# First and last feature tiles of each FFN input product go whole in three passes; operand sums are made later

## The chip, the cores and the metric

The kernel runs on one core of one Trainium2 chip. The metric is the device time of one execution in microseconds (us). Before the change it is 2356.58 us, the median of 3 runs that lie between 2354.08 and 2357.6.

## The reference

Two layers of a hybrid trunk for 512 tokens of width 1024, batch 1, all in fp32. Each layer holds two SwiGLU feed-forward networks (FFNs) of width 2816, one before and one after a mixing part; the sublayers read the same residual `h`.

```python
def swiglu_ffn(x, w_in, w_out):
    g, u = jnp.split(x @ w_in, 2, axis=-1)      # w_in 1024 x 5632
    return (jax.nn.silu(g) * u) @ w_out         # w_out 2816 x 1024
# per layer
h = h + 0.5 * swiglu_ffn(rms_norm(h, n1), ffn1_w_in, ffn1_w_out)
h = h + mixing(rms_norm(h, n2))                 # SSD heads and latent attention, one output projection
h = h + 0.5 * swiglu_ffn(rms_norm(h, n3), ffn2_w_in, ffn2_w_out)
h = h + sigmoid(rms_norm(h, n4) @ w_g) * (p @ w_p)
```

The change touches `x @ w_in` of the four FFNs and nothing else.

## The kernel before

Activations lie transposed, features on the 128 partitions and the 512 tokens along the free axis, in slots of 128x512 fp32. The residual is eight such slots, `h[0]` to `h[7]`. The factor of the RMS norm (one number per token) is put on after the product, so a product needs only `h` times the gain.

**Three passes.** TensorE multiplies in fp32r, which keeps fewer bits than fp32. Every operand is therefore split into a rounded half `hi` (a cast on ACT) and the rest `lo` (a subtraction on DVE), and each product is the sum of hi·hi, hi·lo and lo·hi: `acc_wx` (L408 to L410) for whole tiles, `product` (L584 to L586) for quarter products.

**Weights.** All weights pass through one list of units in program order. A unit is 128x1024 (512 KB). `load_one` fetches it with a DMA on SP's queue; `split_one` makes `hi` (L290) and `lo` (L291); `weights()` keeps the splits two units ahead of the product that asks. There are 6 raw buffers, 3 for `hi`, 3 for `lo`, 8 PSUM banks and 71 slots.

**Quarter products.** `x @ w_in` goes by a Strassen-Winograd scheme: the tokens are cut into two halves of 256 (`HT`), the 8 tiles of depth into 4 pairs, and four feature tiles (a group) into two pairs. Seven products of 24 matmuls of 128x256 each take the place of eight. The weight operands of products 1, 2 and 3 are quarters as loaded. Those of 5 and 7 are the quarter of 1 or 3 with another quarter added to it: POOL issues an accumulating DMA for that (L304), which waits until the split of the earlier quarter has read the buffer. Those of 6 and 4 come from an addition on DVE (L301). The 22 gate and 22 up tiles make 11 groups: five of gate, five of up, taking turns, and a mixed one, "m", of the last two gate and two up tiles. `ORDER` sets the order of the products of a group; products 7 and 4 of a group come between those of the next.

**Operands of the quarter products.** `NormQ` takes the eight tiles `h[k]` as they become final. For each pair it makes two scaled tiles on ACT (L529), four sums of 128x256 on DVE (L548, L550, L551, L554), and for each of seven operands a `hi` on ACT (L421) and a `lo` on DVE (L422). The running sum of squares for the norm goes beside it (L468, L469); `stats` and `spread` turn it into the factor with a few small matmuls. For layer 0's first FFN the input is transposed on TensorE first (L1453).

**Seams.** At the start of an FFN input product all seven operand families are made while the first products run. At its end, the gated tiles are split for the output product (`split_pair`, again L421 and L422), and the product `"o"` begins with `w_out`.

**Order.** Each engine runs its instructions in one queue, in an order that a scheduler fixed when the kernel was built, from the program order and its own simulation of the times. An instruction that waits holds up everything behind it on its engine. In layer 0 two small loads are read by such instructions early in the kernel: `a_log` by ACT, and `pos_i` by the DVE cast `pf` (L717).

Of the kernel before, what the change touches and what calls it, by code (L numbers as in the profile page):

```python
# [91 lines left out]
def kernel(ctx: ExitStack, tc: tile.TileContext, a: dict, out: bass.AP):  # L92
# [50 lines left out]
    def plan_ffn(i, nm, w_in, w_out):  # L143
        wq = w_in.rearrange("(k two p) f -> two p k f", two=2, p=P)

        def quarter(n, kh, c):
            x, q = GROUPS[n]
            c0 = q * 4 * P
            if x == "m":
                return [(slice(g * P, (g + 1) * P), wq[kh, :, :, g * FF + c0 + c * P:g * FF + c0 + (c + 1) * P])  # L150
                        for g in range(2)]
            c0 += (x == "u") * FF + c * 2 * P
            return [(slice(0, 2 * P), wq[kh, :, :, c0:c0 + 2 * P])]
# [362 lines left out]
    class NormQ(Norm):  # L516

        def __init__(self, *args):  # L520
            super().__init__(*args)
            self.O = {p: [] for p in range(1, 8)}
            self.pair = []

        def add_operand(self, src, operand=True):
            w = self.gain(self.k)
            self.k += 1
            x = S()
            A.activation(x.ap, src, AF.Copy, scale=w)  # L529
            self.pair.append(x)  # L530
            if len(self.pair) == 2:
                e, o = self.pair
                self.pair = []
                self.quarters(e, o)
                slots.put(e, o)

        def quarters(self, e, o):
            a11, a21, a12, a22 = e[:, :HT], e[:, HT:], o[:, :HT], o[:, HT:]
            s, t = S(), S()
            s1, s2, s3, s4 = s[:, :HT], s[:, HT:], t[:, :HT], t[:, HT:]  # L540
# [5 lines left out]
            ready(1, a11)  # L546
            ready(2, a12)
# [8 lines left out]
            ready(4, a22)  # L556
            slots.put(s, t)

        def drop_product(self, p):
            slots.put(*self.O.pop(p))  # L560
# [7 lines left out]
    def ffn(i, nm, norm, nxt, start=lambda: None, tables=lambda: None, between=lambda: None):  # L568

        hid = [[], []]
        NG = len(GROUPS)

        def product(bank, n, p, first):
            hi, lo = weights((i, nm, n, p))
            ops = norm.O[p]
            for k in range(4):
                x = ops[k]
                for f in range(2):  # L580
# [3 lines left out]
                    mm(o, lhsT=hi[:, k, cs], rhs=x[:, :HT], start=first and f == k == 0, stop=False, **more)  # L584
                    mm(o, lhsT=hi[:, k, cs], rhs=x[:, HT:], start=False, stop=False, **more)  # L585
                    mm(o, lhsT=lo[:, k, cs], rhs=x[:, :HT], start=False, stop=f == 1 and k == 3, **more)  # L586
# [7 lines left out]
        def finish(n, a, c, src):  # L594
# [48 lines left out]
        live = {}
        for n in range(NG + 1):
            cur = live[n] = {}
            old = live.get(n - 1)
            if n < NG:
                if GROUPS[n][0] != "u":
                    for a in range(2):
# [864 lines left out]
```

## Time and profile before

| | |
|---|---|
| median of 3 runs | 2356.58 us |
| profiled execution | 2355.45 us, span 2353.7 us, mean granted TensorE clock 0.987 |
| TensorE matmul | 2288.2 us busy, 97% of the span |
| DVE | 1613.9 us, 69% |
| ACT | 1131.5 us, 48% |
| FFN input products | 0 to 250, 765 to 990, 1183 to 1405 and 1921 to 2148 us |

The profiled execution is 1.1 us below the median of the runs. A matmul's busy time is modelled, so a row of matmuls counts as busy from end to end; a stall shows only where a stretch has fewer matmuls than fit in it. The granted clock (PEclk) is 1.00 at full speed and 0.50 at half.

### The profile page before, as it was taken

To read this page: it belongs to the slowest core of one execution; us is meant where nothing else is said; L and a number is where in the kernel's file an instruction comes from. 1 tells how busy PE (TensorE), PEld (TensorE's weight loads), DVE (VectorE), ACT (ScalarE), POOL (GpSimd) and SP (SyncE) were. 2 spreads that over 40 slices of the span, in tenths; PEclk is the share of its full clock that TensorE was granted. 3 is DMA by queue.
4 is the path that set the end of the run, shared out by engine and by line. 5 is a ranking of instruction groups with operands and counts; after the bars stand their busy time and mean duration, and the time that the engine had idled before them with its cause. 6 is when DMAs were issued, how large, how long until landed. Compare 5 with 4: busy or idle time off the path is not lost.

```text
span 2353.7 us, 35460 instructions
## 1 busy us (share of the span) xinstructions
PE 2288.2 (97%) x14118; PEld 2047.7 (87%) x14118; DVE 1613.9 (69%) x2544; ACT 1131.5 (48%) x1861; POOL 242.8 (10%) x232
## 2 busy tenths in 40 slices
PE   7999999999999899999999999999999989999998
PEld 6999888878888899988899988888788879998887
DVE  7777645688666877844687784466876777777345
ACT  6545424454555655532564563254544555455224
POOL 1111000123000111100011110011320001111000
PEclk8999999999999899999999999999999999999999
DMA  5666334311221566543256563342112226665332
GB/s 120 153 135 128 100 94 115 94 51 40 71 62 57 117 135 135 115 117 87 85 126 133 128 127 99 83 118 81 34 48 77 71 54 136 134 135 119 92 86 72
DMA packets 339826, 233.30 MB, mean 99 GB/s; under 512 B 20462, under 2 KB 334028, under 8 KB 339660
## 3 DMA queue, kind: packets, MB, share of 16 engines
q1 hardware_dynamic: 288972, 184.89, 26.6%
q0 software_dynamic: 50688, 46.14, 13.3%
q8 instruction: 111, 1.82, 0.3%
q14 instruction: 55, 0.45, 0.1%
HBM read 228.90 MB, written 2.10 MB: 98 GB/s over the span
## 4 chain that ended last, share of the span: by engine, by line
PE 87%; DVE 5%; issue 3%; DMA 2%; ACT 2%; POOL 1%; SPq 0%; ACTq 0%; POOLq 0%
PE b L408 14%; PE b L410 14%; PE b L409 14%; PE b L584 11%; PE b L585 11%; PE b L586 11%; DMA raw<-in_ffn_w_in_dram 2%; PE b L416 1%; PE b L417 1%; PE b L418 1%; DVE lo L291 1%; ACT hi L290 1%; PE b L1054 1%; DVE s L422 1%; PE b L1219 1%
## 5 line engine op out<-in xcount | busy, mean ns | idle before, releaser
L290 ACT CAST hi<-raw 128x1024 fp32r<-128x1024 f32 (+3 forms) x560 | 549.7, 982 | 838.7 <-PE b L409 380.4
L291 DVE TENSOR_TENSOR lo<-raw,hi 128x1024 fp32r<-128x1024 f32 (+3 forms) x560 | 641.9, 1147 | 434.7 <-ACT hi L290 434.1
L584 PE MATMUL b<-s,hi 128*128 128x256 f32 x2464 | 706.8, 288 | 21.7 <-ACT hi L290 13.0
L585 PE MATMUL b<-s,hi 128*128 128x256 f32 x2464 | 704.9, 287 | 8.1 <-DVE s L422 8.1
L586 PE MATMUL b<-s,lo 128*128 128x256 f32 x2464 | 697.0, 286 | 8.6 <-DVE lo L291 8.6
L408 PE MATMUL b<-s,hi 128*128 128x512 f32 (+1 forms) x1498 | 591.7, 397 | 11.2 <-ACT hi L290 11.2
L410 PE MATMUL b<-s,lo 128*128 128x512 f32 (+1 forms) x1498 | 583.9, 390 | 0.0
L409 PE MATMUL b<-s,hi 128*128 128x512 f32 (+1 forms) x1498 | 583.3, 390 | 0.0
L584 PEld LDWEIGHTS b<-s,hi 128*128 128x128 f32 x2464 | 481.4, 195 | 27.6 <-ACT hi L290 16.0
L585 PEld LDWEIGHTS b<-s,hi 128*128 128x128 f32 x2464 | 482.0, 196 | 10.0 <-DVE s L422 9.3
L586 PEld LDWEIGHTS b<-s,lo 128*128 128x128 f32 x2464 | 477.8, 195 | 9.1 <-DVE lo L291 9.0
L408 PEld LDWEIGHTS b<-s,hi 128*128 128x128 f32 x1498 | 281.3, 188 | 69.1 <-ACT hi L290 12.0
L410 PEld LDWEIGHTS b<-s,lo 128*128 128x128 f32 x1498 | 280.8, 187 | 58.5
L409 PEld LDWEIGHTS b<-s,hi 128*128 128x128 f32 x1498 | 281.2, 188 | 57.7 <-issue 2.9
L304 POOL DMA_DIRECT2D raw<-in_ffn_w_in_dram x96 | 124.0, 1336 | 1003.6 <-DVE lo L291 883.5
L421 ACT CAST s<-s 128x256 fp32r<-128x256 f32 (+1 forms) x304 | 110.7, 416 | 35.5 <-PE b L586 10.7
L422 DVE TENSOR_TENSOR s<-s,s 128x256 fp32r<-128x256 f32 (+1 forms) x304 | 117.5, 432 | 3.6 <-ACT s L421 2.6
L421 ACT CAST s<-b 128x128 fp32r<-128x128 f32 (+2 forms) x196 | 67.2, 361 | 99.7 <-DVE s L422 38.7
L301 DVE TENSOR_TENSOR raw<-raw,raw 128x1024 f32<-128x1024 f32 x88 | 107.6, 1223 | 2.1
L422 DVE TENSOR_TENSOR s<-b,s 128x128 fp32r<-128x128 f32 (+2 forms) x196 | 76.0, 402 | 30.1 <-ACT s L421 28.9
L493 POOL TENSOR_TENSOR nr<-nv,half 128x4 f32<-128x4 f32 (+1 forms) x14 | 16.7, 1190 | 642.4 <-DVE nv L485 639.1
L614 ACT COPY s<-b 128x512 f32<-128x512 f32 x132 | 76.6, 581 | 10.3 <-PE b L586 10.3
(244 smaller groups left out, 2236.1 us busy)
## 6 DMA issues: line engine op xcount, KB each, us to landing
raw<-in_ffn_w_in_dram SPq DMA_DIRECT2D x120, 512.0 KB
raw<-in_ffn_w_in_dram POOLq DMA_DIRECT2D x80, 512.0 KB, 5.8
raw<-in_ffn_w_out_dram SPq DMA_DIRECT2D x64, 512.0 KB
raw<-in_w_in_mix_dram SPq DMA_DIRECT2D x50, 512.0 KB
raw<-in_w_out_mix_dram SPq DMA_DIRECT2D x32, 512.0 KB
raw<-in_ffn_w_out_dram SPq DMA_DIRECT2D x32, 384.0 KB
raw<-in_w_ple_gate_dram SPq DMA_DIRECT2D x16, 512.0 KB
raw<-in_ffn_w_in_dram SPq DMA_DIRECT2D x24, 256.0 KB
```

What stands on the lines that cost most here:

```text
L290: A.copy(hi[:, :n], x[:, :n])
L291: V.tensor_tensor(lo[:, :n], x[:, :n], hi[:, :n].bitcast(F32), op=ALU.subtract)
L301: V.tensor_tensor(x[:, :n], x[:, :n], loaded[add][:, :n], op=ALU.add)
L304: lambda dst, src: G.dma_start(out=dst, in_=src, accum_op=ALU.add))
L408: mm(b, lhsT=hi[:, kk, cs], rhs=xh, start=st, stop=False)
L409: mm(b, lhsT=hi[:, kk, cs], rhs=xl, start=False, stop=False)
L410: mm(b, lhsT=lo[:, kk, cs], rhs=xh, start=False, stop=en)
L421: A.copy(hi, src)
L422: V.tensor_tensor(lo, src, hi.bitcast(F32), op=ALU.subtract)
L584: mm(o, lhsT=hi[:, k, cs], rhs=x[:, :HT], start=first and f == k == 0, stop=False, **more)
L585: mm(o, lhsT=hi[:, k, cs], rhs=x[:, HT:], start=False, stop=False, **more)
L586: mm(o, lhsT=lo[:, k, cs], rhs=x[:, :HT], start=False, stop=f == 1 and k == 3, **more)
```

## The change

Of the 22 gate and 22 up tiles, eight no longer go by quarter products. Gate tiles 0 to 3 go first, each "whole": 24 matmuls of 128x512 with `acc_wx`, from a weight unit of eight depth tiles by 128 columns. The last two gate and two up tiles (20 and 21) go whole at the end, in turn with products 7 and 4 of the last group. Nine groups of quarter products stay, and the mixed group is gone. The first group now runs 1, 5, 2, 3, 6 rather than 1, 2, 5, 3, 6.

For the whole tiles the eight `h[k]` are split as they are (`hi` on ACT, `lo` by one DVE operation of 128x512, now L457). Operands 1, 2 and 4 are plain halves of these tiles, so they need nothing more. Operands 5, 3, 6 and 7 are made from `h` by `sums`, called once after each of the four first whole tiles. In the changed kernel, the lines are L418 to L420 for whole tiles, L591 to L593 for quarter products, L300 and L301 for the weight splits, L431 and L432 for the halves, L538 and L547 to L553 in `sums`.

```diff
+GROUPS = [("u", 0)] + [(x, q) for q in range(1, KF // 4) for x in "gu"]
+NG = len(GROUPS)
+LAST = KF // 4 * 4
+
+FIRST_ORDER = ((1, 0), (5, 0), (2, 0), (3, 0), (6, 0))
 ORDER = ((1, 0), (2, 0), (7, 1), (5, 0), (4, 1), (3, 0), (6, 0))
-GROUPS = [(x, q) for q in range(KF // 4) for x in "gu"] + [("m", KF // 4)]
...
+        def whole(x, f):
+            unit((i, nm, x, f), KD, P, (None, kview(w_in, 0, KD, (x == "u") * FF + f * P, P)))
+
+        for f in range(4):
+            whole("g", f)
+        for n in range(NG):
+            for p, back in ORDER if n else FIRST_ORDER:
+                quarter_unit(n - back, p)
+        quarter_unit(NG - 1, 7)
+        whole("g", LAST)
+        quarter_unit(NG - 1, 4)
+        whole("g", LAST + 1)
+        whole("u", LAST)
+        whole("u", LAST + 1)
...
-            self.O = {p: [] for p in range(1, 8)}
-            self.pair = []
-
-        def add_operand(self, src, operand=True):
...
+            self.O = {p: [] for p in (5, 3, 6, 7)}
+
+        def sums(self, j):
+            e, o, s, t = S(), S(), S(), S()
+            for k, x in ((2 * j, e), (2 * j + 1, o)):
+                A.activation(x.ap, h[k].ap, AF.Copy, scale=self.gain(k))
...
-            ready(1, a11)
-            ready(2, a12)
             V.tensor_tensor(s1, a21, a22, op=ALU.subtract)
             ready(5, s1)
...
-            ready(4, a22)
-            slots.put(s, t)
+            slots.put(e, o, s, t)
+
+        def operand(self, p, k):
+            if p in self.O:
+                y = self.O[p][k]
+                return y[:, :HT], y[:, HT:]
+            odd, half = {1: (0, 0), 2: (1, 0), 4: (1, 1)}[p]
+            hi, lo = self.X[2 * k + odd]
+            ts = slice(half * HT, (half + 1) * HT)
+            return hi[:, ts], lo[:, ts]
...
+        for f in range(4):
+            held.append((f, whole("g", f)))
+            if f == 0:
+                start()
+                norm.stats()
+            if f == 2:
+                norm.spread()
+            if f >= 2:
+                while held:
+                    evac(*held.pop(0))
+            norm.sums(f)
...
+        product(ba, NG - 1, 7, False)
+        combined(NG - 1, 1, 1, ba, cur["n5"], ALU.subtract, swap=True)
+        presplit(1)
+        g = [whole("g", LAST)]
+        presplit(2)
+        product(ba, NG - 1, 4, False)
+        finish(NG - 1, 1, 0, ba.ap)
```

`whole` in `ffn` takes a bank and runs `acc_wx` on the unit; `evac` multiplies a bank by the norm's factor into the gated tiles and puts SiLU on them.

**How the order moves, first place: TensorE at the start of layer 0's second FFN.** In these rows `b` is a PSUM bank, `s` an operand slot, `hi` and `lo` a weight's halves. Before, the last whole-tile product of the mixing part (L410) is followed by quarter products 1 and 2:

```order
L410 MATMUL b_282_7725<-s_489_7482,lo_7560 128x512
L408 MATMUL b_282_7725<-s_489_7482,hi_7559 128x512
L409 MATMUL b_282_7725<-s_490_7483,hi_7559 128x512
L410 MATMUL b_282_7725<-s_489_7482,lo_7560 128x512
L584 MATMUL b_283_7775<-s_496_7529,hi_7630 128x256
L585 MATMUL b_283_7775<-s_496_7529,hi_7630 128x256
L586 MATMUL b_283_7775<-s_496_7529,lo_7631 128x256
L584 MATMUL b_283_7775<-s_496_7529,hi_7630 128x256
```

Now (bank `b_285` is gate tile 0, `b_287` tile 1, `b_288` tile 2) three whole tiles share the first operand slots as these come ready:

```order
L418 MATMUL b_285_7475<-s_494_7351,hi_7381 128x512
L418 MATMUL b_287_7537<-s_489_7304,hi_7429 128x512
L419 MATMUL b_287_7537<-s_490_7305,hi_7429 128x512
L419 MATMUL b_285_7475<-s_495_7352,hi_7381 128x512
L420 MATMUL b_285_7475<-s_494_7351,lo_7382 128x512
L418 MATMUL b_285_7475<-s_496_7372,hi_7381 128x512
L419 MATMUL b_285_7475<-s_497_7373,hi_7381 128x512
L420 MATMUL b_285_7475<-s_496_7372,lo_7382 128x512
L418 MATMUL b_285_7475<-s_498_7399,hi_7381 128x512
L418 MATMUL b_288_7590<-s_489_7304,hi_7478 128x512
L419 MATMUL b_288_7590<-s_490_7305,hi_7478 128x512
```

The matmuls became twice as wide and reuse each operand three times before a quarter product is reached.

**Second place: ACT at the end of layer 0's first input product.** Before, `hi_2880` is the weight of product 7 of the mixed group, `hi_2920` that of product 4, `hi_2968` the first unit of the output product:

```order
L290 CAST hi_2880<-raw_2527 128x1024
L421 CAST s_156_3042<-s_110_2203 128x256
L421 CAST s_156_3042<-s_112_2205 128x256
L421 CAST s_154_2998<-s_111_2204 128x256
L290 CAST hi_2920<-raw_2364 128x1024
L421 CAST s_152_2996<-s_109_2202 128x256
L421 CAST s_152_2996<-s_111_2204 128x256
L421 CAST s_160_3057<-s_119_2658 128x256
L421 CAST s_158_3044<-s_110_2203 128x256
L421 CAST s_158_3044<-s_112_2205 128x256
L290 CAST hi_2968<-raw_2592 128x1024
```

Now `hi_2495` is the weight of product 7 of the last group (it reads what the accumulating DMA leaves), `hi_2525` that of whole gate tile 20:

```order
L300 CAST hi_2495<-raw_2195 128x1024
L431 CAST s_145_2787<-s_97_1645 128x256
L431 CAST s_145_2787<-s_99_1647 128x256
L608 ACTIVATE s_108_2098<-s_108_2098 128x512
L431 CAST s_132_2685<-s_86_1192 128x256
L431 CAST s_132_2685<-s_88_1194 128x256
L300 CAST hi_2525<-raw_2258 128x1024
```

The cast for product 7 is followed by casts for product 4 and the four whole tiles, and no longer by the output product's.

**Third place: DVE at the start of layer 0.** Before, the cast `pf` stands directly ahead of the weight split `lo_338` of product 5:

```order
L422 TENSOR_TENSOR s_47_288<-s_43_281,s_47_288 128x256
L422 TENSOR_TENSOR s_39_259<-s_33_242,s_39_259 128x256
L422 TENSOR_TENSOR s_52_307<-s_43_281,s_52_307 128x256
L551 TENSOR_TENSOR s_45_284<-s_43_281,s_44_283 128x256
L717 CAST pf_800<-pos_i 4x128
L291 TENSOR_TENSOR lo_338<-raw_97,hi_337 128x1024
```

Now the split of gate tile 2 (`lo_247`) stands ahead of it, and the next split behind it is that of gate tile 3:

```order
L301 TENSOR_TENSOR lo_247<-raw_222,hi_246 128x1024
L547 TENSOR_TENSOR s_44_387<-s_42_385,s_43_386 128x256
L479 TENSOR_TENSOR s_33_300<-s_33_300,tmp_302 128x512
L432 TENSOR_TENSOR s_38_339<-s_36_334,s_38_339 128x256
L432 TENSOR_TENSOR s_40_347<-s_36_334,s_40_347 128x256
L549 TENSOR_TENSOR s_44_387<-s_44_387,s_42_385 128x256
L432 TENSOR_TENSOR s_39_344<-s_37_335,s_39_344 128x256
L479 TENSOR_TENSOR s_33_300<-s_33_300,tmp_305 128x512
L553 TENSOR_TENSOR s_66_517<-s_63_514 128x256
L775 CAST pf_934<-pos_i 4x128
```

`pf` has moved from behind the splits of two quarter products to behind those of three whole tiles.

More of the change, by code (lines that the diff above doesn't have):

```diff
@@ L147, in quarter @@
             x, q = GROUPS[n]
[L148 to L152, printed above, removed]
+            c0 = q * 4 * P + (x == "u") * FF + c * 2 * P
             return [(slice(0, 2 * P), wq[kh, :, :, c0:c0 + 2 * P])]
@@ L639, in presplit, with whole @@
                 q = len(H) // 2
-                if q < done[0] and len(slots.free) - 4 - (KF - len(hid[0]) * 2) >= KEEP:
+                if q < done[0] and len(slots.free) - 4 - (LAST - len(hid[0]) * 2) >= KEEP:
                     split_pair(q)
[L643 to L649, printed above, removed]
-                        hid[a] += [S() for _ in range(1 if GROUPS[n][0] == "m" else 2)]
-                ba = cur["a"] = B()
-                product(ba, n, 1, True)
-                cur["m1"] = copied(ba)
-                bc = B()
-                product(bc, n, 2, True)
-                if n:
+        def whole(x, f):
+            b = B()
+            acc_wx(b.ap, weights((i, nm, x, f)), norm.ops)
+            return b
@@ new lines, in ffn, with evac @@
+        held = []
+        def evac(f, b):
+            q, fs = f // 2, slice(f % 2 * HT, (f % 2 + 1) * HT)
+            if f % 2 == 0:
+                for a in range(2):
+                    hid[a].append(S())
+            for a in range(2):
+                ts = slice(a * HT, (a + 1) * HT)
+                V.tensor_tensor(hid[a][q][:, fs], b[:, ts], norm.rb[:, ts], op=ALU.mult)
+            banks.put(b)
+            if f % 2:
+                for a in range(2):
+                    A.activation(hid[a][q].ap, hid[a][q].ap, AF.Silu)
@@ new lines, in ffn @@
+        for f in range(4):
[9 more added lines that the diff above has]
+            norm.sums(f)
+        cur = {}
+        for n in range(NG):
+            old, cur = cur, {}
+            if GROUPS[n][0] == "g":
+                for a in range(2):
+                    hid[a] += [S(), S()]
+            for p, back in ORDER if n else FIRST_ORDER:
+                if p == 1:
+                    ba = cur["a"] = B()
+                    product(ba, n, 1, True)
+                    cur["m1"] = copied(ba)
+                elif p == 2:
+                    bc = B()
+                    product(bc, n, 2, True)
@@ L690, in ffn, with split_last @@
+        def split_last():
+            for f in range(2):
+                t, hi, lo = hid[f].pop(), S(F32R), S(F32R)
+                halves(t.ap, hi.ap, lo.ap)
+                slots.put(t)
+                H[LAST + f] = hi, lo
         for m in range(KD):
@@ L695, in ffn @@
                 if m == 0:
-                    while len(H) < k0 + nk:
+                    while len(H) < min(k0 + nk, LAST):
                         split_pair(len(H) // 2)
+                    if k0 + nk == KF:
+                        split_last()
                 acc_wx(b.ap, w, {f: (p.ap, q.ap) for f, (p, q) in H.items()}, k0, k0 == 0, k0 + 8 >= KF)
```

103 lines of the change are left out of this document (44 added, 59 removed).

## The prediction

> **What bounds the kernel now.** First the page: busy shares, the chain, the clock by slices.
>
> ```profile
> PE 2288.2 (97%) x14118; PEld 2047.7 (87%) x14118; DVE 1613.9 (69%) x2544; ACT 1131.5 (48%) x1861; POOL 242.8 (10%) x232
> PE 87%; DVE 5%; issue 3%; DMA 2%; ACT 2%; POOL 1%; SPq 0%; ACTq 0%; POOLq 0%
> ```
>
> TensorE sets the time almost everywhere. Two prices therefore matter: that of a matmul in a full stretch, and that of the stretches that are not full. The view by windows gives both (columns: window in us, then length, busy time and count of each engine, granted clock, DMA share, GB/s).
>
> ```profile
> 810.00:980.00 170.00, 170.00 (x1419) 170.00 (x1418) 129.99 (x146) 88.32 (x117) 23.11 (x18) 1.00 0.62 134
> 300.00:360.00 60.00, 60.00 (x266) 49.71 (x265) 24.21 (x28) 16.93 (x21) 0.00 (x0) 1.00 0.35 94
> ```
>
> The first lies inside an FFN input product and holds 256-wide matmuls: 170/1419 = 0.1198 us each, with nothing lost. The second is an output product: 60/266 = 0.2256 us per 512-wide matmul. The steady state has nothing to give. These are the eight seams, the starts and the ends of the four input products:
>
> ```profile
> 14.00:82.00 68.00, 54.69 (x407) 52.75 (x406) 52.59 (x101) 40.55 (x71) 6.55 (x6) 0.90 0.49 113
> 765.00:805.00 40.00, 32.30 (x223) 30.87 (x223) 36.16 (x69) 27.55 (x53) 3.60 (x3) 0.83 0.49 107
> 1183.00:1203.00 20.00, 17.53 (x136) 16.36 (x135) 15.55 (x25) 11.51 (x19) 4.09 (x4) 1.00 0.52 97
> 1920.00:1961.00 41.00, 32.99 (x224) 31.66 (x223) 36.94 (x70) 28.20 (x55) 3.87 (x4) 0.83 0.47 105
> 222.00:270.00 48.00, 43.62 (x322) 41.86 (x322) 38.30 (x66) 27.88 (x55) 6.47 (x5) 0.96 0.54 120
> 985.00:1013.00 28.00, 24.75 (x166) 23.04 (x165) 23.77 (x45) 14.68 (x32) 2.61 (x2) 0.94 0.57 141
> 1390.00:1426.00 36.00, 30.14 (x200) 28.32 (x200) 27.80 (x52) 17.99 (x39) 2.59 (x2) 0.91 0.39 96
> 2140.00:2170.00 30.00, 25.42 (x174) 23.68 (x173) 25.03 (x46) 15.05 (x32) 2.62 (x2) 0.94 0.55 132
> ```
>
> A seam's loss is its length less its matmuls at 0.1198. Starts: 68 - 407 x 0.1198 = 19.2; likewise 13.3, 3.7 and 14.2; together 50.4 us. The ends also hold the output product's first 512-wide matmuls; these are the rows of its hi·hi line (L408) alone in the same windows:
>
> ```profile
> 222.00:270.00 48.00, 3.62 (x9) 1.89 (x10) 0.96 0.54 120
> 985.00:1013.00 28.00, 3.63 (x9) 1.70 (x9) 0.94 0.57 141
> 1390.00:1426.00 36.00, 4.14 (x10) 1.98 (x10) 0.91 0.39 96
> 2140.00:2170.00 30.00, 3.35 (x8) 1.51 (x8) 0.94 0.55 132
> ```
>
> Three passes each make 27, 27, 30 and 24 wide matmuls. Loss of the first end: 48 - 295 x 0.1198 - 27 x 0.2256 = 6.6; the others 5.3, 8.9 and 6.6; together 27.4. **All seams lose 77.8 us.** That is the pot from which any gain must come.
>
> Two causes fill it. In layer 0's start, the queues of ACT and DVE stand still for small loads (timeline; idle time before and its releaser in brackets; then the window behind it):
>
> ```profile
> 27.03 0.22 ACT L843 ACTIVATE d_a<-a_log 128x16 f32<-128x16 f32 x1 [4.37 <-DMA a_log<-in_a_log_dram]
> 29.76 0.21 ACT L843 ACTIVATE d_a<-a_log 128x16 f32<-128x16 f32 x1 [1.91 <-DMA a_log<-in_a_log_dram]
> 30.64 0.21 DVE L717 CAST pf<-pos_i 4x128 f32<-4x128 int32 x1 [6.34 <-DMA pos_i<-in_positions_dram]
> 32.05 0.58 PE L586 MATMUL b<-s,lo 128*128 128x256 f32 x1 [7.83 <-DVE lo L291]
> 32.00:41.40 9.40, 8.87 (x40) 8.56 (x41) 7.89 (x18) 2.48 (x4) 1.29 (x1) 0.50 0.35 53
> ```
>
> The weight split that TensorE needs is queued behind `pf`, so TensorE idles 7.83 us and then runs at a granted clock of 0.50 for over 9 us: 40 matmuls in 9.40 us are 0.235 each, nearly twice the pitch. In the second FFN of both layers the operand families are the cause:
>
> ```profile
> 765.00:775.00 10.00, 6.15 (x29) 5.41 (x29) 10.00 (x25) 8.99 (x23) 0.00 (x0) 0.67 0.53 106
> 775.00:785.00 10.00, 6.65 (x47) 6.25 (x46) 10.00 (x23) 6.67 (x15) 0.00 (x0) 0.84 0.16 52
> ```
>
> DVE is busy 10.00 of 10 us while TensorE gets through 29 and 47 matmuls of the 83 that fit.
>
> **The change: columns.** Each FFN loses 2 x 7 x 24 = 336 matmuls of 256 (11 groups to 9) and gains 8 x 24 = 192 of 512. 192 x 0.2256 - 336 x 0.1198 = 43.3 - 40.2 = 3.06 us, times four: **+12.2 us**, certain, as TensorE is the bound.
>
> **Starts of the second FFNs.** What DVE must do before product 5, from the groups of 757 to 793 us, the kernel-wide group of L447 (count | busy us, mean ns), that window's DVE time, and the first and last starts of two lines:
>
> ```profile
> L422 DVE TENSOR_TENSOR s<-s,s 128x256 fp32r<-128x256 f32 x28 | 10.4, 417 | 0.0
> L291 DVE TENSOR_TENSOR lo<-raw,hi 128x1024 fp32r<-128x1024 f32 x7 | 8.5, 1217 | 0.0
> L1289 DVE TENSOR_TENSOR s<-b,s 128x512 f32<-128x512 f32 x8 | 5.1, 684 | 5.1 <-PE b L410 5.1
> L469 DVE TENSOR_TENSOR s<-s,tmp 128x512 f32<-128x512 f32 x7 | 4.8, 683 | 0.0
> L301 DVE TENSOR_TENSOR raw<-raw,raw 128x1024 f32<-128x1024 f32 x2 | 2.4, 1214 | 0.0
> L554 DVE TENSOR_TENSOR s<-s 128x256 f32<-128x256 f32 x4 | 1.7, 419 | 0.0
> L548 DVE TENSOR_TENSOR s<-s,s 128x256 f32<-128x256 f32 x4 | 1.7, 418 | 0.0
> L550 DVE TENSOR_TENSOR s<-s,s 128x256 f32<-128x256 f32 x4 | 1.7, 417 | 0.0
> L551 DVE TENSOR_TENSOR s<-s,s 128x256 f32<-128x256 f32 x4 | 1.7, 416 | 0.0
> L619 DVE TENSOR_TENSOR s<-b,s 128x512 f32<-128x512 f32 x1 | 0.7, 682 | 0.0
> L447 DVE SCALAR_TENSOR_TENSOR s<-s,vec,s 128x512 fp32r<-128x512 f32 x32 | 24.1, 752 | 22.2 <-ACT s L446 22.2
> 757.00:793.00 36.00, 34.26 (x69) 0.81 0.35 73
> L1289 DVE TENSOR_TENSOR s<-b,s x8: 681/682/693, 756.6 to 767.4; 128x512 f32<-128x512 f32 x8
> L584 PE MATMUL b<-s,hi x4: 277/281/384, 765.1 to 767.1; 128*128 128x256 f32 x4
> ```
>
> After: 8 residual updates at 0.684, 7 weight splits at 1.217, 8 `lo` of whole tiles at 0.752, 7 squares' sums at 0.683, 16 sums of 256 and 16 `lo` of 256 at 0.417, in all 38.1 us. Neighbours overlap: the 69 instructions of the window add up to 38.7 us by their groups and occupy 34.26, a factor 0.885, so 33.7 us. The cover on TensorE is the rest of the mixing product (the first update starts at 756.6, the first quarter product at 765.1: 8.5), 96 whole matmuls (21.7) and product 1 (2.9): 33.1 us. So DVE is about level with TensorE where it was far behind. What stays: the order above takes three whole tiles in turn, so the `hi` casts of tiles 2 and 3, behind `h` and square work on ACT, come some 2.4 and 1.4 us late. Product 5 now runs second, and its weight needs an accumulating DMA behind product 1's split: 5.8 to 7.6 us to landing in this place now,
>
> ```profile
> DMA to landing us min/median/max: 5.8/7.6/7.6
> ```
>
> so cast and split end 2.4 to 4.2 us after TensorE is ready for it; I take 3.3. With 1.4 for half clock (between 0 and the 3.3 that 10 us at 0.67 lose now): **8.5 us for each such start, against 13.3 and 14.2**; 4 if the waits lie under each other, 13 if DVE runs later than its sum.
>
> **Start of layer 0.** SP's order keeps the small loads in the same place, so `pf` still ends near 30.6. Only gate tile 3's split is now queued behind it, not product 5's. Tiles 0 to 2 give TensorE 72 x 0.2256 = 16.2 us from 14 on, to about 30. Tile 3's cast, on ACT behind both `a_log` waits, ends near 33 and its `lo` near 36: a stall of 5 to 6 us in place of 7.8, and some half clock after it. I take **10 against 19.2**; 6 if the casts slip through, 14 if the half clock lasts as it does now. **Layer 1's first FFN** has its last output tiles as cover and no `pos_i`: 1.5 (0 to 3) against 3.7.
>
> **The ends.** Now TensorE finishes 7, then 4, then needs the output product's `hi`, behind pairs that are split late; the longest waits there:
>
> ```profile
> PE b L408 <- ACT hi L290: 11.2, 4, 4.1
> 242.00:252.00 10.00, 8.27 (x55) 7.87 (x54) 10.00 (x21) 3.87 (x9) 2.60 (x2) 0.83 0.59 99
> ```
>
> After, 96 whole matmuls give 21.7 us in which the pairs are split, so that wait goes. What is late next is tile 20: on ACT its cast stands behind product 7's, which waits for the accumulating DMA. Counted from the start of product 5 on TensorE: product 3's `lo` ends at 2.5, the DMA lands 5.8 to 7.1 later (8.6 to 9.9 with its issue), tile 20's `lo` ends at 14 to 15.2. Products 5, 4, 3, 6 (4 x 24 x 0.1198 = 11.5) and none else run till then, so TensorE waits 2.5 to 3.7 us less what tile 20's first passes may do on `hi` alone: 2 to 3.2, say 2.6. The window 242 to 252 shows the clock at 0.83 although its longest wait is 1.1 us, a loss of 1.7, of which I take half, 0.9: **3.5 us for each end, 14 for four, against 27.4** (0.8 each with an early landing and full clock; 5 with 3.2 of wait and the whole 1.7).
>
> [...]
>
> **Sum.** Starts 10 + 8.5 + 8.5 + 1.5 = 28.5, ends 14: 42.5 of the 77.8 remain, a gain of 35.3; less 12.2 for columns: -23.1. The profiled execution's 2355.45 us becomes 2332.4; with the 1.1 by which the median is above it, **2333 us**. Costed at nothing: SP loads 35 weight units of 512 KB per FFN in place of 33, POOL 18 in place of 22, so fewer bytes in all, and the DMA share in the steady windows is at most 0.62; operands hold 32 slots in place of 28 (8 tiles and 4 families of four, before 7 families), which could only delay pair splits, and these have 21.7 us of cover.
>
> **Rivals.**
>
> *The seams close.* The low ends: 6 + 4 + 4 + 0 for the starts, 0.8 each at the ends, 17.2 remain: 2356.6 + 12.2 - 60.6 = 2308. For it: 21.7 us of cover at both sides is more than any wait. Against it: ACT and DVE queues are fixed, and a cast behind a DMA waits whatever the cover.
>
> *Slower: the late accumulating DMA in front of tile 20.* Place: ACT's cast of product 7 at the four ends. The DMA waits for product 3's `lo` on DVE, which is 10.00 of 10 busy there now. If pair splits (L431, L432) run ahead of that `lo` and it comes 6 us later, TensorE waits 2.6 + 6 and then pays a clock window of 3.4: 12 us per end. Total 28.5 + 48 = 76.5 remain, the gain is 1.3 and the time 2367. It decides from 9.3 us per end on: (77.8 - 12.2 - 28.5)/4. Against it: in DVE's order two pair splits stand shortly ahead of that `lo`, and eight between it and product 7's.
>
> *No change.* The ends keep their 27.4 because the DMA holds them, the second FFNs' starts their 27.5 because DVE is as full as now; only layer 0 and the short start gain, 11.4 against 12.2: 2357.
>
> **Chances.** Forecast (own range 2318 to 2349, from the ends of its terms) 0.62; seams close 0.20; slower 0.12; no change 0.06. The 80% range must take in half of the second case and the fourth: 2311 to 2357 leaves out about 0.1 below and 0.1 above. What a measurement here can tell from no change is 0.2%, 4.7 us. Faster 0.82, same 0.06, slower 0.12.
>
> **What would show it.** In the profile after: some 194 us of 256-wide matmuls per FFN at 0.12 and 192 wide ones at 0.226, or the 12.2 is wrong. `pf` near 30.6 with a wait of 5 to 6 us on `lo` before it ends, or layer 0's term is. DVE near 10 of 10 from 757 to 790 with TensorE above 8 of 10, or the level sum is. At the ends, one wait of 2 to 3 us of L418 on ACT's `hi` and none at the output product; a wait over 9 us there would make the prediction wrong.

## The result: 0.7% faster, and where the time went

The changed kernel takes 2338.9 us in the median of 8 runs (2333.85 to 2346.76); the kernel before takes 2354.52 us in 8 runs beside them (2353.15 to 2357.75). The ratio is 0.9934, 95% interval 0.9917 to 0.9951: 15.6 us faster by the medians, where a gain of 23 (2333 from 2356.6) was forecast. The runs of the changed kernel spread over 13 us, those of the kernel before over 5. The profiled execution is the second longest of the eight, 2346.55 us with a span of 2344.9, so in it the change is worth only 8.8 us. That will matter below.

The page of the changed kernel: busy shares, the chain of waits and the transfers.

```profile
span 2344.9 us, 34036 instructions
PE 2295.8 (98%) x13542; PEld 2021.8 (86%) x13542; DVE 1552.6 (66%) x2456; ACT 1093.3 (47%) x1780; POOL 215.5 (9%) x208
...
PE 81%; issue 10%; DVE 4%; DMA 2%; ACT 2%; POOL 1%; SPq 1%; POOLq 0%; ACTq 0%; DVEq 0%
...
raw<-in_ffn_w_in_dram SPq DMA_DIRECT2D x140, 512.0 KB
raw<-in_ffn_w_in_dram POOLq DMA_DIRECT2D x72, 512.0 KB, 5.9
```

TensorE is still the bound, DVE and ACT have less to do, and POOL makes its 72 accumulating loads. The list of TensorE's waits says what it waits for now:

```profile
PE b L591 <- ACT hi L300: 9.9, 6, 4.5
PE b L418 <- ACT hi L300: 7.8, 7, 1.9
PE b L420 <- DVE lo L301: 6.5, 7, 1.9
PE b L591 <- ACT s L608: 6.4, 6, 2.5
```

The list of the kernel before was led by thirteen waits of quarter products for ACT's casts, the output product's waits for them, and waits for DVE's `lo`, of which product 5's at layer 0's start was 7.8 us:

```profile
PE b L584 <- ACT hi L290: 13.0, 13, 2.6
PE b L408 <- ACT hi L290: 11.2, 4, 4.1
PE b L586 <- DVE lo L291: 8.6, 2, 7.8
```

The output product's waits and the long one of product 5 at layer 0 are gone, and of the first kind six are left, one of them 4.5 us long. New are short waits of the whole tiles (L418, L420) and, in the fourth row, waits of a quarter product that no seam explains.

To see where the difference lies, every profile here was put into the same ledger. For each matmul the time to the next one's start, less its pitch (0.1198 us for 256 columns, 0.2256 for 512), is its loss; the losses are added up over the starts, the middles and the ends of the four input products. (The windows are somewhat wider than the prediction's, so the kernel before stands here at 56 + 29 rather than 50 + 27.)

| loss in us | starts | middles | ends | elsewhere | all | span less loss |
|---|---|---|---|---|---|---|
| before | 56.3 | 1.2 | 29.2 | 83.9 | 170.3 | 2183.4 |
| changed | 37.6 | 12.2 | 15.0 | 84.8 | 149.4 | 2195.5 |
| difference | -18.7 | +11.0 | -14.2 | +0.9 | -20.9 | +12.1 |

-20.9 + 12.1 = -8.8, the difference of the spans. So the columns cost 12.1 us, the two kinds of seam gave 32.9 back, and **11 us appeared in a place where the kernel before lost next to nothing: the middle of the input products**. Two windows of the changed kernel show it, the middle of layer 0's and of layer 1's first FFN:

```profile
75.00:215.00 140.00, 140.00 (x1169) 140.00 (x1168) 110.90 (x137) 73.31 (x99) 18.00 (x14) 1.00 0.61 132
1200.00:1370.00 170.00, 164.25 (x1346) 163.03 (x1345) 123.92 (x140) 83.09 (x108) 20.55 (x16) 0.99 0.56 121
```

140/1169 is 0.1198 us per matmul, the full pitch. In the second window 1346 matmuls ran where 1419 fit: 73 x 0.1198 = 8.7 us are lost. Six groups there lose 0.4 to 1.2 us each in one wait, at full clock. A seventh loses 2.65 us at 1349 us, and behind it the granted clock is 0.50 for the 3.4 us from 1352.2 to 1355.7, another 1.7 us. TensorE's waits in that window:

```profile
PE b L591 <- ACT s L608: 4.5, 4, 2.5
PE b L591 <- DVE s L620: 1.3, 3, 0.6
```

Both releasers are work that stands on ACT and DVE behind a late weight. The group of ACT's weight casts in the same window, with what ended the idle time before them:

```profile
L300 ACT CAST hi<-raw 128x1024 fp32r<-128x1024 f32 x57 | 59.6, 1047 | 72.5 <-PE b L592 36.3 <-DMA raw<-in_ffn_w_in_dram 28.4 <-issue 7.4
```

The casts wait 28.4 us for loads; in the same product of the kernel before they waited 4.5 us:

```profile
L290 ACT CAST hi<-raw 128x1024 fp32r<-128x1024 f32 x66 | 69.1, 1049 | 86.0 <-PE b L585 66.5 <-issue 8.0 <-DMA raw<-in_ffn_w_in_dram 4.5
```

From the view of the accumulating loads there, first of the kernel before, then of the changed one:

```profile
DMA to landing us min/median/max: 4.5/5.8/6.2
```

```profile
DMA to landing us min/median/max: 5.7/6.7/8.2
```

POOL's timeline has the reason one step further back (start, length, idle time before). First the changed kernel in the undisturbed middle of layer 0's first FFN, then in layer 1's:

```profile
132.79 1.28 POOL L314 DMA_DIRECT2D raw<-in_ffn_w_in_dram  x1 [13.00 <-DVE lo L301]
138.66 1.28 POOL L314 DMA_DIRECT2D raw<-in_ffn_w_in_dram  x1 [4.58 <-DVE lo L301]
152.91 1.28 POOL L314 DMA_DIRECT2D raw<-in_ffn_w_in_dram  x1 [12.97 <-DVE lo L301]
...
1226.28 1.28 POOL L314 DMA_DIRECT2D raw<-in_ffn_w_in_dram  x1 [14.88 <-DVE lo L301]
1230.86 1.28 POOL L314 DMA_DIRECT2D raw<-in_ffn_w_in_dram  x1 [3.30 <-DVE lo L301]
1247.12 1.28 POOL L314 DMA_DIRECT2D raw<-in_ffn_w_in_dram  x1 [14.98 <-DVE lo L301]
```

Each group issues two accumulating loads, for product 7 of the group before and for product 5. In these groups of layer 0 they start 5.9 us apart, about the time one takes to land (median 5.9 us there). In layer 1 they start 4.4 to 4.7 us apart in seven groups running, so the second is under way with the first and takes 7.9 to 8.2 us to land; the casts of the second begin up to 8.3 us after its start rather than 6.0. And the group takes 20.6 to 21.2 us, once 22.2, where it takes 20.1 in layer 0 (152.91 - 132.79).

### The profile page after: what moved, and what is told of

Same layout as the page of the kernel before. It is cut to its first block, busy times and chain, and to the rows that moved or that the text cites. A ratio compares the mean times of both kernels' runs of the same rounds, so it can differ in the third digit from the quotient of the medians.

```text
span 2344.9 us, 34036 instructions
## 1 busy us (share of the span) xinstructions
PE 2295.8 (98%) x13542; PEld 2021.8 (86%) x13542; DVE 1552.6 (66%) x2456; ACT 1093.3 (47%) x1780; POOL 215.5 (9%) x208
## 4 chain that ended last, share of the span: by engine, by line
PE 81%; issue 10%; DVE 4%; DMA 2%; ACT 2%; POOL 1%; SPq 1%; POOLq 0%; ACTq 0%; DVEq 0%
PE b L418 15%; PE b L420 15%; PE b L419 15%; PE b L591 7%; PE b L593 7%; PE b L592 7%; DMA raw<-in_ffn_w_in_dram 2%; PE b L427 2%; PE b L426 2%; PE b L428 2%; DVE lo L301 1%; PE b L1112 1%; ACT hi L300 1%; PE b L1277 1%; DVE s L432 1%
## 5 line engine op out<-in xcount | busy, mean ns | idle before, releaser
L301 DVE TENSOR_TENSOR lo<-raw,hi 128x1024 fp32r<-128x1024 f32 (+3 forms) x536 | 612.4, 1143 | 469.6 <-ACT hi L300 469.0
L300 ACT CAST hi<-raw 128x1024 fp32r<-128x1024 f32 (+3 forms) x536 | 523.8, 979 | 855.6 <-PE b L419 411.5
L418 PE MATMUL b<-s,hi 128*128 128x512 f32 (+1 forms) x1754 | 693.5, 397 | 7.8 <-ACT hi L300 7.8
L420 PE MATMUL b<-s,lo 128*128 128x512 f32 (+1 forms) x1754 | 685.8, 392 | 6.5 <-DVE lo L301 6.5
L419 PE MATMUL b<-s,hi 128*128 128x512 f32 (+1 forms) x1754 | 683.8, 390 | 0.0
L591 PE MATMUL b<-s,hi 128*128 128x256 f32 x2016 | 574.4, 286 | 18.0 <-ACT hi L300 9.9
L592 PE MATMUL b<-s,hi 128*128 128x256 f32 x2016 | 572.0, 284 | 0.0
L593 PE MATMUL b<-s,lo 128*128 128x256 f32 x2016 | 567.9, 285 | 1.7 <-DVE lo L301 1.7
L591 PEld LDWEIGHTS b<-s,hi 128*128 128x128 f32 x2016 | 390.1, 193 | 23.5 <-ACT hi L300 11.7
L418 PEld LDWEIGHTS b<-s,hi 128*128 128x128 f32 x1754 | 330.6, 188 | 77.4 <-ACT hi L300 10.7
L420 PEld LDWEIGHTS b<-s,lo 128*128 128x128 f32 x1754 | 329.9, 188 | 77.6 <-DVE lo L301 8.8
L592 PEld LDWEIGHTS b<-s,hi 128*128 128x128 f32 x2016 | 390.2, 194 | 0.2
L593 PEld LDWEIGHTS b<-s,lo 128*128 128x128 f32 x2016 | 387.2, 193 | 2.6 <-DVE lo L301 2.5
L419 PEld LDWEIGHTS b<-s,hi 128*128 128x128 f32 x1754 | 330.5, 188 | 68.0 <-issue 2.9
L314 POOL DMA_DIRECT2D raw<-in_ffn_w_in_dram x72 | 92.8, 1289 | 850.5 <-DVE lo L301 819.2
L431 ACT CAST s<-b 128x128 fp32r<-128x128 f32 (+2 forms) x196 | 67.2, 361 | 99.8 <-DVE s L432 38.7
L431 ACT CAST s<-s 128x256 fp32r<-128x256 f32 (+1 forms) x248 | 94.2, 423 | 36.8 <-DVE s L611 13.2
L432 DVE TENSOR_TENSOR s<-s,s 128x256 fp32r<-128x256 f32 (+1 forms) x248 | 100.2, 442 | 9.8 <-PE b L593 7.4
L432 DVE TENSOR_TENSOR s<-b,s 128x128 fp32r<-128x128 f32 (+2 forms) x196 | 75.9, 401 | 30.2 <-ACT s L431 29.1
L426 PE MATMUL b<-hi,s 128*128 128x512 f32 (+1 forms) x208 | 78.5, 377 | 0.0
```

The lines of the kernel that those rows point to most:

```text
L300: A.copy(hi[:, :n], x[:, :n])
L301: V.tensor_tensor(lo[:, :n], x[:, :n], hi[:, :n].bitcast(F32), op=ALU.subtract)
L314: lambda dst, src: G.dma_start(out=dst, in_=src, accum_op=ALU.add))
L418: mm(b, lhsT=hi[:, kk, cs], rhs=xh, start=st, stop=False)
L419: mm(b, lhsT=hi[:, kk, cs], rhs=xl, start=False, stop=False)
L420: mm(b, lhsT=lo[:, kk, cs], rhs=xh, start=False, stop=en)
```

## The experiments

### The same kernel, a second profile

No edit.

> The changed kernel, unaltered, looked at once more. In its first profile 13 us were lost in the middle of the input products (9.1 of them in layer 1's first FFN, about 1 us per group), where the kernel before loses nothing. Theory (a): this is a matter of timing between the two accumulating DMAs of a group, a state that a product falls into or not. Then another execution has the loss at another FFN or nowhere, and the time goes with it: about 2334 without it, 2346 with it. Rival (b): it is built into the order of layer 1's first FFN. Then the 9 us come back at the same place.

Measured: 2346.58 us, 149.5 us of loss in all, as it happens the same total. But it lies elsewhere: the middles lose 1.1, 1.9, 3.3 and 1.3 us rather than 0.3, 1.5, 9.0 and 1.4, and the ends 18.7 rather than 15.0. The start of layer 1's first FFN sets its pairs of loads 4.4 to 4.8 us apart again, with this landing time there:

```profile
DMA to landing us min/median/max: 5.8/6.0/8.0
```

So the close spacing comes back at the same place, which favours (b), and its price only in part (3.3, not 9.0), which favours (a). Both expectations had a part right: the spacing belongs to this kernel at this place, and how long the loads then take varies from one execution to the next (median 6.0 us here, 6.7 in the first profile). The time, though, did not fall with the loss in the middle as (a) had it.

### Product 5 third, not second

```diff
-FIRST_ORDER = ((1, 0), (5, 0), (2, 0), (3, 0), (6, 0))
+FIRST_ORDER = ((1, 0), (2, 0), (5, 0), (3, 0), (6, 0))
```

> The first group runs products 1, 2, 5, 3, 6 as it did before the change; all else as changed. Theory: product 5's accumulating DMA is late because it stands second (waits of 4.7 and 4.0 us at the starts of the second FFNs, 1.2 and 0.9 in layer 0); with product 2's 2.9 us ahead of it the starts lose 3 us less in each second FFN and 1.5 less in layer 0, some 7 us in all: 2332. If that late start is also what sets off the loss in the middle, that goes too and the runs lie close together near 2327. Rival: DVE's sums and splits are as late as the DMA, product 2 only takes the wait over: 2338 to 2340.

Measured: 2336.22 us against 2359.2 of the kernel before, ratio 0.9912 (0.989 to 0.9934), runs from 2330.31 to 2347.69. In its profile (2332.11 us) the starts lose 31.2 us (37.6 before this edit), 6.4 less, and the middles 1.0 in all. POOL's timeline in layer 1's first FFN:

```profile
1199.27 1.28 POOL L314 DMA_DIRECT2D raw<-in_ffn_w_in_dram  x1 [11.62 <-DVE lo L301]
1205.03 1.28 POOL L314 DMA_DIRECT2D raw<-in_ffn_w_in_dram  x1 [4.47 <-DVE lo L301]
1219.53 1.28 POOL L314 DMA_DIRECT2D raw<-in_ffn_w_in_dram  x1 [13.22 <-DVE lo L301]
1225.30 1.28 POOL L314 DMA_DIRECT2D raw<-in_ffn_w_in_dram  x1 [4.49 <-DVE lo L301]
```

The loads start 5.8 us apart from the first group on. So product 5 in second place is what sets the close spacing at this place. The 6.4 us at the starts are near the 7 expected, but they can't be put down to this edit: the next two kernels, which keep product 5 second, lose 33 and 29.9 us at their starts. And this kernel's list has waits that the changed kernel's doesn't have, for the norm's factor from POOL and from DVE, so the rival, that product 2 only takes the wait over, is right in part:

```profile
PE b L513 <- POOL nr L503: 5.4, 2, 4.0
PE b L591 <- DVE nv L495: 3.1, 1, 3.1
```

The narrow spread was not found: the runs lie 17 us apart, and the interval overlaps the changed kernel's. By the times this run does not decide what the order is worth.

### Whole tiles 20 and 21 ahead of products 7 and 4

```diff
-        quarter_unit(NG - 1, 7)
         whole("g", LAST)
-        quarter_unit(NG - 1, 4)
+        quarter_unit(NG - 1, 7)
         whole("g", LAST + 1)
+        quarter_unit(NG - 1, 4)
```

(and the same in `ffn`, where the products are issued).

> At the end of each input product whole gate tile 20 goes before product 7, and tile 21 before product 4; all else as changed. Theory: the waits of 1.0 and 1.1 us at each end come from tile 20's cast standing behind product 7's, which waits for its DMA. Now 5.4 us of tile 20 cover that DMA: the ends lose 7 instead of 14.5 us, 2332. Rival: tile 20's own weights or the pair splits are what is late, and the waits stay: 2339.

Measured: 2325.75 us, ratio 0.986 (0.9843 to 0.9877). The ends lose 1.2 us in all, 0.3 each, where 7 was expected and the changed kernel has 15.0. These are the waits of TensorE from 185 to 240 us, first of the changed kernel, then of this one:

```profile
PE b L420 <- DVE lo L301: 1.0, 1, 1.0
PE b L418 <- ACT hi L300: 0.9, 1, 0.9
```

```profile
PE b L591 <- ACT s L431: 0.6, 1, 0.6
```

And its window at that end:

```profile
205.00:240.00 35.00, 34.40 (x239) 32.10 (x238) 31.50 (x56) 24.81 (x49) 1.28 (x1) 1.00 0.53 135
```

The two short waits are gone. The granted clock was 0.95 in the changed kernel's window from 215 to 250 us and is 1.00 here. So at the ends nearly the whole cost was the cast of product 7 ahead of tile 20's. Nearly twice the expected gain came: the stalls at the four ends (8.9 us in the changed kernel, counted from start to start) went, and the half clock behind two of them (3.4 us) with them. The middles still lose 6.8 us, with the loads of layer 1's first FFN 4.4 to 4.7 us apart in its first groups: the edit at the ends does not touch them.

### The first half of the change alone

Gate tiles 0 to 3 whole at the start; the last four tiles by the mixed group, as before the change.

```diff
-GROUPS = [("u", 0)] + [(x, q) for q in range(1, KF // 4) for x in "gu"]
+GROUPS = [("u", 0)] + [(x, q) for q in range(1, KF // 4) for x in "gu"] + [("m", KF // 4)]
...
-        whole("g", LAST)
...
-        whole("u", LAST + 1)
```

> Only the first half of the change: gate tiles 0 to 3 whole at the start, operand sums made later; the last four tiles go by the mixed group as before the change. Columns then cost 96 x 0.2256 - 168 x 0.1198 = 1.5 us per FFN in place of 3.1. Theory: starts and ends are worth what the ledger says, 15 us at the starts and 13 at the ends. So this kernel gains 6 us of columns back and loses 13 at the ends: about 2346. Rival: the ends gain nothing of their own and follow from the starts: 2333.

Measured: 2341.06 us, ratio 0.9925 (0.9912 to 0.9938). Span less loss is 2334.9 - 145.7 = 2189.2, so the columns cost 5.8 us here (6.1 expected, 12.1 with the whole change). The ends lose 25.5 us, 10.5 more than in the changed kernel. That is the theory's side: the ends do not follow from the starts. The middles lose 7.7, and the starts 29.9, 7.7 less than in the changed kernel with the same first group. Product 5's load at the second FFNs' starts landed after 7.5 and 8.1 us here and after 10.4 and 9.7 there; why it did, no run explains. By the times the second half of the change, as it was written, is worth nothing that can be told (0.9925 against 0.9934): its 10.5 us at the ends pay for its 6.3 us of columns and little more.

### Product 5's quarter by a plain load

```diff
+                if p == 1:
+                    at[n, "b"] = raw(4, 256, *quarter(n, 0, 1))
...
-(at[n, before][0], quarter(n, 0, 1) if add is None else at[n, add][1])))
+(at[n, before][0], at[n, "b"] if p == 5 else quarter(n, 0, 1) if add is None else at[n, add][1])))
```

The order 1, 5, 2, 3, 6 is kept. Product 5's second quarter comes on SP's queue and is added on DVE; only product 7 has an accumulating load left.

> The changed kernel, order 1, 5, 2, 3, 6 kept, but product 5's second weight quarter comes by a plain load on SP and an addition on DVE; only product 7 keeps an accumulating DMA. Theory: the loss in the middle (12 us in one profile, 8 in another) comes from the two accumulating DMAs of a group when they are issued 4.7 us apart and so overlap (landing up to 8 us), which then repeats from group to group; 5.9 us apart, they don't. With one such DMA per group the middle loses 1 us or less in all, and product 5's wait at the second FFNs' starts (4.7, 4.0) falls below 2: about 2322 to 2328, and DVE has 9 additions of 1.22 us more per FFN, which it has room for (77% busy in the middle). Rival: the loss comes from ACT's and DVE's queues, whatever feeds them; then the middle still loses 5 us or more, and the additions make it worse: 2340 or above.

Measured: 2316.33 us, ratio 0.9836 (0.9822 to 0.9849). The middles lose 0.8 us, the second FFNs' starts 4.5 each (12.0 and 11.8 in the changed kernel), the ends 13.3. The two middles (the second is layer 1's first FFN):

```profile
75.00:215.00 140.00, 140.00 (x1169) 140.00 (x1168) 119.99 (x148) 73.73 (x103) 8.98 (x7) 1.00 0.52 132
1190.00:1340.00 150.00, 150.00 (x1252) 150.00 (x1251) 123.89 (x133) 75.01 (x95) 8.98 (x7) 1.00 0.53 134
```

150/1252 is 0.1198: the full pitch at the place that lost 9 us. DVE is busy 124 of 150 us and hides the additions. The rival falls: the queues are as full as they were or fuller (in layer 1's first FFN DVE 83% and ACT 50% busy, 73% and 49% in the changed kernel), and without a second accumulating load nothing is lost. It also says what the loss at the second FFNs' starts mostly was: product 5's accumulating load, not DVE's work. The gain of 23 us beside the changed kernel's 2338.9 is more than the 11 to 17 expected, since layer 0's start gained as well (12.8 to 7.4).

### Both orders

The first and the second edit above together.

> Both orders together: the first group runs 1, 2, 5, 3, 6, and whole tiles 20 and 21 go before products 7 and 4. Theory: the parts add, since one acts at the starts and in the middle and the other at the ends. In the profiles taken the first left 31 us at the starts and 1 in the middle, the second 1 at the ends; the changed kernel had 38, 12 and 15. So 32 us under the changed kernel: 2310 to 2318 beside 2355 to 2359 of the kernel before. Rival: the first order only moved the loss about by chance; then the middle loses 5 to 10 again and this is 2322 to 2328.

Measured: 2317.62 us, ratio 0.9841 (0.9827 to 0.9854), runs from 2316.46 to 2321.82. Starts 33.2, middles 1.0, ends 1.2. The middle of layer 1's first FFN:

```profile
1186.00:1336.00 150.00, 150.00 (x1252) 150.00 (x1251) 115.31 (x126) 76.39 (x98) 19.27 (x15) 1.00 0.59 125
```

POOL's timeline there:

```profile
1210.44 1.28 POOL L314 DMA_DIRECT2D raw<-in_ffn_w_in_dram  x1 [13.22 <-DVE lo L301]
1216.21 1.28 POOL L314 DMA_DIRECT2D raw<-in_ffn_w_in_dram  x1 [4.50 <-DVE lo L301]
```

5.8 us apart again, and nothing lost. With the first order the middles lost 1.0, 1.0 and 1.2 us in the three profiles that have it; with product 5 second and two accumulating loads 12.2, 7.6, 6.8 and 7.7. These profiles speak for the first order; by the times its worth isn't shown, since the interval of this ratio still touches that of the second edit alone (0.9843 to 0.9877). Nor does the order keep every pair apart: in layer 0's second FFN two pairs here start 4.7 and 4.6 us apart, with landings of 7.4 and 6.5 us, and nothing is lost there. At the starts the parts did not add: 33.2 rather than 31. The wait for the norm's factor from POOL in the second FFNs is here too:

```profile
PE b L513 <- POOL nr L503: 5.7, 2, 4.2
```

### The small loads early

```diff
-            small_load(t, a[nm][i:i + 1, :].to_broadcast([P, HS]))
+            (G.dma_start if nm == "a_log" else small_load)(out=t, in_=a[nm][i:i + 1, :].to_broadcast([P, HS]))
...
-    small_load(pos_i, a["positions"].rearrange("b (c p) -> (b c) p", p=P))
+    G.dma_start(out=pos_i, in_=a["positions"].rearrange("b (c p) -> (b c) p", p=P))
```

on top of both orders.

> As the kernel with both orders, and a_log and pos_i are loaded on POOL's queue at the start in place of SP's queue behind weights. Theory: in layer 0's start DVE stands still until pos_i lands at 29 us and ACT until a_log at 26 and 28; tile 3's split is late for that, with the half clock that follows. Without it layer 0's start loses 5 us less (12 to about 7): 2306 to 2313. Rival: what is late there is the DVE work itself (8 splits, 16 sums), as in the second FFN, and nothing changes: within 2 us of the kernel with both orders.

Measured: 2312.88 us, ratio 0.9816 (0.9803 to 0.983). Layer 0's start loses 6.6 us, 5.7 less than with both orders alone (2.0 of the 6.6 is a wait at 10.0 us in the transposes, which lay just ahead of the ledger's window there). `pf` runs at 12.7 us instead of 29.1 and waits for nothing. The theory held at that start. The whole kernel gained 4.7 us, not more, since the start of layer 0's second FFN lost 11.7 us in place of 8.1: the wait for POOL's `nr` there is 3.9 us in place of 1.5, which no run explains.

### All three edits on the changed kernel

Tiles ahead of products 7 and 4, product 5 by a plain load (order 1, 5, 2, 3, 6), small loads early.

> The changed kernel with three of the edits at once: tiles 20 and 21 ahead of products 7 and 4, product 5's second quarter by SP and a DVE addition (order 1, 5, 2, 3, 6 kept), and a_log and pos_i loaded early by POOL. Theory: each acts on its own seam. Ends 1 us in all (as with the first alone, 13 with the second alone), middle 1, the second FFNs' starts 4.5 each (as with the second alone), layer 0's start about 6: 15 us under the kernel with the plain load alone, 2300 to 2305. Rival: the ends need the DVE room that the additions take (9 more of 1.22 us per FFN), or POOL and SP loads collide; then the ends keep 5 us or more, or layer 0's start 10: 2308 to 2314.

Measured: **2300.14 us** (2298.66 to 2300.64), ratio 0.9765 (0.9751 to 0.9778), the fastest kernel here and 39 us under the changed one. Starts 3.8 + 4.5 + 1.0 + 5.6, middles 0.8, ends 1.2.

The page's busy shares:

```profile
PE 2277.4 (99%) x13542; PEld 2011.6 (88%) x13542; DVE 1596.5 (69%) x2492; ACT 1095.8 (48%) x1780; POOL 170.9 (7%) x175
```

TensorE's largest wait that is left in the input products:

```profile
PE b L420 <- ACT hi L302: 3.8, 2, 1.9
```

It is two waits of 1.9 us of a whole tile for ACT's cast, one at each second FFN's start. Of the 86 us of loss outside the input products nothing was touched.

### The kernel before, with the small loads early

The last edit alone, put on the kernel before the change.

> The kernel before the change, with a_log and pos_i loaded early on POOL's queue, all else as before. Theory: its stall of 7.8 us at 24 us and the half clock behind it (22 us lost at that start) come from ACT's and DVE's waits for these two loads, not from the seven operand families. Then that start loses 8 to 12 us less: 2344 to 2349 beside 2355 to 2359. Rival: DVE is full there with the families as in the second FFNs (which lose 13 to 14 without any such load), so that start still loses 14 or more: 2350 to 2356.

Measured: 2345.06 us, ratio 0.9959 (0.9947 to 0.9972). Layer 0's start loses 11.9 instead of 22.5 us. The window that held 407 matmuls holds 492:

```profile
14.00:82.00 68.00, 62.74 (x492) 60.87 (x492) 63.20 (x115) 47.59 (x82) 10.14 (x8) 0.97 0.62 142
```

So half of that start's loss was the two small loads and could be had without the change: 10.6 us, against the 9.7 that the change gained there.

This profile also bounds what was said of the order. The kernel before runs products 1, 2, 5 and lost next to nothing in its middles; with the same order, this one loses 1.1 and 2.3 us in the middles of layer 1's two FFNs. Two pairs of loads in the first of them and two in the second start 4.6 to 4.7 us apart, and these are the landings in the first:

```profile
DMA to landing us min/median/max: 4.6/6.1/8.0
```

So the close spacing does not need product 5 second.

## Why the prediction was right, and where it was not

The direction, the case that was called likeliest, and the range held: 2338.9 in 2311 to 2357, 6 us from the 2333 named. The gain itself, 15.6 us beside the kernel before, is two thirds of the 23 forecast, and in the profiled execution it is 8.8: columns and ends came as forecast, the starts gave 18.7 us of 21.9, and the middle took 11.0 that were not in the sum. By its steps:

**Columns: right.** +12.2 forecast; 12.1 by the ledger, and 5.8 for half the change.

**Ends: right in size, and in the cause that was named next.** 14 us left were forecast, 15.0 and 18.7 measured. The output product's wait went, as forecast, and tile 20's cast behind product 7's took its place; moving it took the ends to 1.2. The waits were shorter than forecast (0.85 and 0.98 us rather than one of 2.6), so the rival that had 12 us per end was right about the place and far from the 9.3 us at which it would have decided. The 3.4 us that this rival adds for the clock are the length of the stretch that the kernel before spent at half clock from 246.2 us on, behind a wait of 1.1 us:

```profile
246.20:249.65 3.45, 3.45 (x18) 3.45 (x18) 3.45 (x7) 0.71 (x2) 2.39 (x2) 0.51 0.57 70
```

The prediction put the loss of that stretch at 1.7 us (10 us at 0.83), so with one such stretch the rival comes to 10.3 us per end, still above 9.3. The clock term stood at 0.9 us per end. In the profile after, two ends have 0.95 in their windows of 35 and 33 us, a loss of about 1.7 each, and two have 1.00: 0.9 on average, behind waits of at most 1.0 us.

```profile
215.00:250.00 35.00, 33.06 (x188) 28.64 (x187) 25.93 (x48) 19.50 (x41) 0.00 (x0) 0.95 0.49 129
960.00:990.00 30.00, 28.20 (x177) 24.85 (x176) 25.78 (x48) 18.96 (x40) 0.49 (x1) 1.00 0.54 141
```

**Start of layer 0: right in sum, in part by luck.** 9.2 us of gain forecast, 9.7 measured. `pf` ran at 29.07 us, 4.70 us late for its load, and TensorE's wait behind it went from 7.83 us to this row of the waits from 11 to 75 us:

```profile
PE b L420 <- DVE lo L301: 1.9, 1, 1.9
```

The wait is shorter than the 5 to 6 us forecast, and the half clock came all the same, 0.83 in the next 10 us:

```profile
32.00:42.00 10.00, 7.98 (x31) 6.45 (x32) 8.77 (x19) 4.17 (x12) 1.47 (x1) 0.83 0.61 143
```

What brings the sum back to the forecast was not in it: product 5's accumulating load is late here too. TensorE waits 0.93 and 0.76 us for its halves at 46 us, and the granted clock is 0.50 again from 48.3 to 51.8 us. With the plain load this start lost 7.4 us rather than 12.8. Layer 1's first FFN lost 1.0 at its start (1.5 forecast).

**Starts of the second FFNs: right in kind, half in size.** Forecast gains of 4.8 and 5.7 us, measured 2.3 and 3.1. The level sum of DVE against TensorE held, though one figure in it is off: the factor 0.885 divides by busy times of groups, in which overlaps are already taken out. The 69 instructions last 40.2 us one by one, so the factor is 0.85 and DVE's work 32.5 us, not 33.7. Three windows of the changed kernel, at the place where TensorE got through 29 and 47 matmuls before (many are 512 wide now):

```profile
756.00:766.00 10.00, 8.10 (x36) 6.40 (x35) 10.00 (x21) 10.00 (x18) 0.00 (x0) 1.00 0.35 107
766.00:776.00 10.00, 9.99 (x45) 7.85 (x43) 10.00 (x24) 6.29 (x15) 0.00 (x0) 1.00 0.28 89
776.00:786.00 10.00, 9.47 (x56) 8.01 (x54) 4.33 (x8) 1.45 (x4) 1.33 (x1) 1.00 0.82 209
```

DVE is at 10.00 of 10 in the first two, as before, but it has room again from some 778 us on, not from 790; and TensorE is covered, but for a wait of 1.90 us for tile 2's cast (2.4 + 1.4 forecast for tiles 2 and 3). The mis-sized terms are product 5's load and the clock behind it. The load was put at 2.4 to 4.2 us, with 3.3 taken; TensorE's timeline has:

```profile
762.32 0.50 PE L418 MATMUL b<-s,hi 128*128 128x512 f32 x1 [1.90 <-ACT hi L300]
790.63 0.58 PE L591 MATMUL b<-s,hi 128*128 128x256 f32 x1 [4.50 <-ACT hi L300]
```

4.50 us, just above the top of that range (from the last matmul's start to the next one's, 4.66 over the pitch), and a granted clock of 0.50 from 789.0 to 795.9 us, of which the 5.2 us behind the wait lose 2.6 where 1.4 was put. The reason is in the landings of the changed kernel's accumulating loads, where 5.8 to 7.6 us were taken for this place:

```profile
DMA to landing us min/median/max: 5.6/5.9/10.4
```

The 10.4 is this load, started at 779.0 us; layer 1's took 9.7. The DMA share there is 0.82, as the last window above shows, but no run tests whether that slows it. With the plain load these starts lose 4.5.

**The middle: the step that failed.** The prediction said that the steady state has nothing to give, and costed the transfers at nothing since there are fewer bytes. It did not ask whether the steady state could be made to lose. Two accumulating loads per group fit with little to spare: mostly 5.4 to 5.9 us apart, some 5.8 to 5.9 us to land. That the first group now runs 1, 5 moves them 4.4 us apart at the start of layer 1's first FFN, and the late load of product 5 delays the splits behind it, so that the next pair is close again. That the loss needs two such loads is shown by the two kernels with one, which lose 0.8 us there in all. That the order sets the spacing is shown for layer 1's first FFN alone (4.4 to 4.8 us in the first groups of the four profiles with product 5 second, 5.7 to 5.9 in the three with it third); elsewhere pairs come 4.7 us apart under either order. That the delayed splits hand it on from group to group is read from the spacing alone and was not tested by itself. Of the 11 us in the first profile this is most; without it the profiled execution would be 2335.5, 3.1 from the 2332.4 of the sum. Nearly half of the 9.0 us in layer 1's first FFN is one group's wait of 2.65 us and the half clock behind it. What stays open is why the same spacing cost 9.0 us there, 3.3 in the second profile, 2.6 with the tiles moved and 3.8 with the first half alone, and what in the other executions makes up the spread of 13 us: of those there is no trace.

## What to carry to other kernels

A full stretch has a price too: before a change near it is costed at nothing, ask how close its transfers run to their limit, since in the first profile here loads that had landed just in time, 5.9 us apart, made a group take 20.6 to 21.2 us rather than 20.1, round after round, once they started 4.4 to 4.7 us apart. Where a queue holds an instruction that waits for a transfer, put work that waits for nothing ahead of it: exchanging two whole tiles with two products took the ends from 15 us to 1, more than the 10 us that the rebuilding of those ends had saved. And small loads deserve a look first: two of them cost the kernel before 10.6 us.

## What the runs showed of the hardware that was not expected

Of two accumulating loads of 512 KB that started 4.4 to 4.7 us apart, the second took up to 8.2 us to land, though not always: in the kernel before the one at 107.4 us, 4.8 us behind the other, took 5.8. Where it started 5.9 us behind the other, at 138.7 us of the changed kernel, it took 5.9. The two kernels with one such load per group, and the three with product 5 third in the first group after the whole tiles, ran their middles at the full pitch but for some 1 us in all. Behind two waits of about 1 us TensorE ran 3.4 us at half clock at some ends (waits of 1.0 and 0.9 us, 0.50 from 225.8 to 229.3 us, 0.95 over 35 us) and not at others of the same kernel (waits of 1.0 and 0.7 us, 1.00 over 30 us).
